# Second block's scores in two matmuls per head, with the high and low part of a value sharing the rows

## The chip, the cores and the metric

One core of a Trainium2 chip runs the whole program. The metric is device time in microseconds (us), lower is better. TensorE (PE) multiplies, VectorE (DVE) and ScalarE (ACT) do elementwise work, GpSimd (POOL) the rest, SyncE (SP) issues the transfers of the weights.

## The reference

Two models run one after the other over 256 tokens of width 2048. The change touches the second one only: two layers, each with four kinds of attention ("mixers") of eight heads of 64 columns.

```python
def second_block(x, norm_gain, w_in, q_norm_gain, k_norm_gain, forget_bias, w_out):
    for layer in range(DEPTH):
        h = rms_norm_2(x, norm_gain[layer])
        proj = jnp.einsum('bsd,dc->bsc', h, w_in[layer])
        ...
        o_a = dilated_attention(apply_rope_2(head_rms_norm(q[0], qn[0]), cos, sin), ..., v[0])
        o_b = stick_breaking_attention(q[1], k[1], v[1])
        o_c = moba_attention(apply_rope_2(head_rms_norm(q[2], qn[1]), cos, sin), ..., v[2])
        o_d = forgetting_attention(head_rms_norm(q[3], qn[2]), head_rms_norm(k[3], kn[2]), v[3], log_f)
        y = y * jax.nn.silu(gate)
        x = x + jnp.einsum('bsc,cd->bsd', y, w_out[layer])
```

## The kernel before, in words

Every operand is kept as two fp32r tiles, a high part and a low part, and a product is three matmuls (`mm3`: high by high, high by low, low by high). Weights arrive by SP's queue in pieces of 1024 columns, ACT casts each to its high part (`wh`), DVE subtracts to get the low part (`wl`).

The second block (`block2`) takes the mixers in the order 1, 0, 2, 3 (stick-breaking, dilated, moba, forgetting). In each it goes over four pairs of heads, i = 0 to 3; a pair fills the 128 partitions with two heads of 64. For every other pair `values` computes the value tiles of two pairs. `qkg` computes q, k and the gate of a pair: three products of 48 matmuls each (tile `p`, one of four PSUM tiles of that name). In mixers 0, 2 and 3 `qk` then normalizes q and k: squares on ACT, two matmuls into tile `hms` on PE, logarithm and exponential on ACT, four steps on POOL (tile `hrt`), a scaling on DVE; in mixers 0 and 2 `rope` follows (one product on POOL, four copies of 32 partitions on ACT, two steps on DVE). The result is split into a high and a low tile (`qkh`, `qkl`). So there are 8 stick-breaking pairs and 24 softmax pairs in all; 16 of those go through `rope`, 8 don't.

`attend` does the attention of a pair. The two heads share the partitions, so one operand must hold zeros where the other head is: `diag` copies parts of the high and low tile into padded tiles (`dph`, `dpl`), two copies on POOL and two on DVE each for q and for k. `soft` makes the scores (tiles `s`) in nine matmuls of 256 columns, `softmax` goes over DVE, ACT and DVE again (tile `e`), six transposes bring the probabilities back into `s`, and `split2` splits them (tile `p` of L858 and L189). The output `o` takes three matmuls of 512 columns and three of 256. `stick` has nine matmuls of 256 columns for its scores and the same six for its output. The projections back to the width of 2048 (`out_proj`, groups of 12 matmuls, `p<-yh,wh` and so on) of the mixer before stand between the pairs.

No order is written out by hand: a scheduler places each engine's instructions from the program's dependences and its own model of time, and the engines then run these lists strictly in order.

Of the kernel before, what the change touches and what calls it, by code (L numbers as in the profile page):

```python
# [9 lines left out]
F32 = mybir.dt.float32  # L10
F32R = mybir.dt.float32r
AF = mybir.ActivationFunctionType
ALU = mybir.AluOpType
# [40 lines left out]

def halves(x, n):
    return x.rearrange("p (j c) -> p j c", c=n)


def block(pair, j):
    return [t[:, j * 128:j * 128 + 128] for t in pair]  # L60


class Lazy:
# [12 lines left out]
class Net:  # L76
# [114 lines left out]
    def split(self, x, name, n, p=slice(0, 128), tag="s"):  # L191
        nc = self.nc
        h = self.slot(name + "h", F32R, tag=tag)
        l = self.slot(name + "l", F32R, tag=tag)
        nc.scalar.copy(h[p, 0:n], x)
        self.sub(l[p, 0:n], x, h[p, 0:n])
        return h, l
# [428 lines left out]
    def block2(self, l, st, rb, first_done, after):  # L626
        nc, a = self.nc, self.a
# [21 lines left out]
            return t  # L649

        NC = None
        self.diagpad(4)
        Y = {}

        def values(mx, hf):
            out = []
            ft = []
            c = 264 if mx == 3 and hf == 0 else 256
            src = a[f"vf{l}"] if c == 264 else a[f"v{l}"][(1, 0, 2, 3).index(mx) * 2 + hf - (mx == 3)]
            ws = [self.wblock(src[b], 8 * c, 4 * c) for b in range(2)]  # L660
            for tt in range(2):
                p = self.ps()[:, 0:c]
                ts = slice(tt * 128, tt * 128 + 128)
                for k in range(KD):
                    xh, xl = X[k]
                    self.mm3(p, (xh[:, ts], xl[:, ts]), self.wcol(ws[k // 8], (k % 8) * c, c), k == 0, k == KD - 1)
                if c == 264:
                    ft.append(self.small.tile([128, 8], F32, tag="ft", name="ft"))
                    nc.vector.tensor_scalar(ft[tt], p[:, 256:264], rcol()[:, tt:tt + 1], None, ALU.mult)
                p = p[:, sl]  # L670
                vh = self.slot("vh", F32R)[:, sl]
                vl = self.slot("vl", F32R)[:, sl]
                rc = rcol()[:, tt:tt + 1]
                nc.scalar.activation(vh, p, AF.Copy, scale=rc)  # L674
                nc.vector.scalar_tensor_tensor(vl, p, rc, vh.bitcast(F32), ALU.mult, ALU.subtract)
                out.append((vh, vl))
            return out, ft

        def qkg(mx, i):
# [19 lines left out]

        def attend(mx, i, q, k, g, v):  # L700
            o = self.pa("o2")
            c = slice((i % 2) * 128, (i % 2) * 128 + 128)
            hv = [[t[:, c] for t in x] for x in v]
            if mx == 1:
                p0, p1 = self.stick(q, k, masks)
            else:
                p0, p1 = self.soft(q, k, masks, NC if mx == 3 else None, i)
            self.mm3(o, hv[0], p0, True, False)
            self.mm3(halves(o, 256)[:, :, 128:256], hv[1], p1, False, True)
            yh, yl = Y[mx][i]  # L710
            t = self.slot("yt", tag="a")[:, sl]
            for j in range(2):
                R = slice(j * 64, j * 64 + 64)
                nc.vector.tensor_tensor(t[R], o[R, j * 256:j * 256 + 256], g[R], ALU.mult)
            nc.scalar.copy(yh, t)
            self.sub(yl, t, yh)

# [46 lines left out]
    def qk(self, l, mx, qk, p, rb):  # L764
        nc = self.nc
        n = SEQ
        sl = slice(0, n)
        t = self.tmp("qkt")[:, sl]
        if mx == 1:
            if qk == 0:  # L770
                nc.vector.scalar_tensor_tensor(t, p, 0.125, rb()[:, sl], ALU.mult, ALU.mult)  # L771
            else:
                nc.vector.tensor_tensor(t, p, rb()[:, sl], ALU.mult)
            return self.split(t, "qk", n)
        nc.vector.tensor_tensor(t, p, rb()[:, sl], ALU.mult)
        v = self.tmp("qsq")[:, sl]
        y = self.tmp("hry")[:, sl]
        r = self.tmp("hrt")[:, sl]
        nc.scalar.activation(v, t, AF.Square)
        vh, vl = self.tmp("qsqh", F32R)[:, sl], self.tmp("qsql", F32R)[:, sl]  # L780
        nc.scalar.copy(vh, v)
        nc.gpsimd.tensor_tensor(vl, v, vh.bitcast(F32), ALU.subtract)
        ms = self.psh.tile([128, 512], F32, tag="h", name="hms")[:, sl]
        nc.tensor.matmul(ms, self.b2const["bd64"], vh, start=True, stop=False)
        nc.tensor.matmul(ms, self.b2const["bd64"], vl, start=False, stop=True)
        self.ln(r, ms, bias=self.eps)
        nc.scalar.activation(v, ms, AF.Identity, bias=self.eps)
        nc.scalar.activation(y, r, AF.Exp, scale=-0.5)
        s = 0.125 if qk == 0 else 1.0
        nc.gpsimd.tensor_tensor(r, v, y, ALU.mult)  # L790
        nc.gpsimd.tensor_tensor(r, r, y, ALU.mult)
        nc.gpsimd.tensor_scalar(r, r, -0.5 * s, 1.5 * s, ALU.mult, ALU.add)
        nc.gpsimd.tensor_tensor(r, r, y, ALU.mult)
        gi = {0: 0, 2: 1, 3: 2}[mx]
        gcol = self.col("qk_gain", (l * 3 + gi) * 2 + qk)
        nc.vector.scalar_tensor_tensor(t, t, gcol, r, ALU.mult, ALU.mult)
        if mx == 3:
            return self.split(t, "qk", n)
        return self.rope(t, self.b2const["rope2c"], self.b2const["rope2s"], n, "qk", (v, y))

    def diagpad(self, n):

        self.dp = []
        self.dpi = 0
        for _ in range(n):
            pr = (self.slot("dph", F32R), self.slot("dpl", F32R))
            for t in pr:
                for j in range(2):
                    self.nc.gpsimd.memset(t[j * 64:j * 64 + 64, 128 - j * 128:256 - j * 128].bitcast(F32), 0.0)
            self.dp.append(pr)  # L810

    def diag(self, x, c):

        pr = self.dp[self.dpi % len(self.dp)]
        self.dpi += 1
        for t, s, eng in zip(pr, x, (self.nc.gpsimd, self.nc.vector)):
            for j in range(2):
                R = slice(j * 64, j * 64 + 64)
                eng.tensor_copy(t[R, j * 128:j * 128 + 128], s[R, c])
        return [t[:, 0:256] for t in pr]  # L820

    def soft(self, q, k, masks, NC, i):

        nc = self.nc
        s0, s1 = self.pa("s0"), self.pa("s1")
        lo, hi = slice(0, 128), slice(128, 256)
        qd = self.diag(q, hi)
        kd = self.diag(k, lo)
        if NC is not None:
            nb = self.slot("nb", F32R, [128, 512], "b")  # L830
            for j in range(2):
                h = 2 * i + j
                nc.gpsimd.tensor_scalar(
                    nb[:, j * 256:j * 256 + 256], NC.bitcast(F32), self.sel[:, h:h + 1], None, ALU.mult)
            nc.tensor.matmul(s0[:, 0:256], self.one, halves(nb, 256)[:, :, lo], start=True, stop=False)
            nc.tensor.matmul(s1, self.one, nb, start=True, stop=False)
        self.mm3(s0[:, 0:256], (q[0][:, lo], q[1][:, lo]), kd, NC is None, True)
        P = []
        for j in range(2):
            P.append([self.softmax(s0[:, j * 128:j * 128 + 128], 128, 128, masks[0])])  # L840
        for j in range(2):
            s = s1[:, j * 256:j * 256 + 256]
            self.mm3(s, block(qd, j), (k[0][:, 0:256], k[1][:, 0:256]), NC is None, NC is None or j == 1)
        for j in range(2):
            P[j].append(self.softmax(s1[:, j * 256:j * 256 + 256], 256, 128, masks[1]))
        I = self.ident
        t0, t1 = s1, s0
        for j in range(2):
            c = j * 256
            nc.tensor.transpose(t0[:, c:c + 128], P[j][0], I)  # L850
            nc.tensor.transpose(t0[:, c + 128:c + 256], P[j][1][:, lo], I)
            nc.tensor.transpose(t1[:, j * 128:j * 128 + 128], P[j][1][:, hi], I)
        return self.split2(t0, 512), self.split2(t1[:, 0:256], 256)
# [8 lines left out]
    def stick(self, q, k, masks):  # L862
# [2 lines left out]
        tri, ones = trir[:, 0:128], trir[:, 128:256]  # L865
        z0, z1 = self.pa("z0"), self.pa("z1")
        lo, hi = slice(0, 128), slice(128, 256)
        qd = self.diag(q, hi)
        kd = self.diag(k, lo)
        for j in range(2):  # L870
            self.mm3(z0[:, j * 256:j * 256 + 256], block(kd, j), (q[0][:, 0:256], q[1][:, 0:256]))
        self.mm3(z1[:, 0:256], (k[0][:, hi], k[1][:, hi]), qd)
        Z, SP = [], []
        for z, m, n in ((z0, strict0, 512), (z1[:, 0:256], strict1, 256)):
            if n == 512:
# [277 lines left out]
```

## Time and profile before

| | |
|---|---|
| time, median of 3 runs | 3187.34 us (3187.2 to 3187.79) |
| the profiled execution's own time | 3187.93 us |
| its span | 3186.2 us |
| mean granted TensorE clock | 0.999 of full speed |
| second block in the trace | 2163 to 3186 us, layers of about 511 us each |

The span runs from the first to the last instruction; 1.7 us of the time lie outside it. In the timelines below, matmuls overlap: the time that one takes in the stream is the distance from its start to the next start, not its printed duration.

### The profile page before, as it was taken

To read this page: it belongs to the slowest core of one execution; us is meant where nothing else is said; L and a number is where in the kernel's file an instruction comes from. 1 tells how busy PE (TensorE), PEld (TensorE's weight loads), DVE (VectorE), ACT (ScalarE), POOL (GpSimd) and SP (SyncE) were. 2 spreads that over 40 slices of the span, in tenths; PEclk is the share of its full clock that TensorE was granted. 3 is DMA by queue.
4 is the path that set the end of the run, shared out by engine and by line. 5 is a ranking of instruction groups with operands and counts; after the bars stand their busy time and mean duration, and the time that the engine had idled before them with its cause. 6 is when DMAs were issued, how large, how long until landed. Compare 5 with 4: busy or idle time off the path is not lost.

```text
span 3186.2 us, 64469 instructions
## 1 busy us (share of the span) xinstructions
PE 3162.5 (99%) x25987; PEld 3142.6 (99%) x25987; DVE 2161.6 (68%) x3673; ACT 1755.1 (55%) x2970; POOL 584.9 (18%) x730
## 2 busy tenths in 40 slices
PE   9999999999999999999999999999999999999999
PEld 8999999999999999999999999999999999999999
DVE  7887655555555678865555555568788778778876
ACT  6666434434344567654444444456677666666764
POOL 1001000000000133310000000023244463144453
PEclk9999999999999999999999999999999999999999
DMA  6343556556565555566565656656555555555554
GB/s 225 117 134 121 179 160 191 177 159 192 157 193 170 174 177 173 166 193 187 169 203 170 203 184 185 191 166 195 171 170 161 176 160 177 157 176 170 167 165 136
DMA packets 165693, 549.43 MB, mean 172 GB/s; under 512 B 18800, under 2 KB 38128, under 8 KB 165392
## 3 DMA queue, kind: packets, MB, share of 16 engines
q1 hardware_dynamic: 163440, 540.70, 54.5%
q0 software_dynamic: 1664, 4.33, 0.5%
q8 instruction: 203, 3.33, 0.4%
q14 instruction: 98, 0.80, 0.1%
q10 hardware_dynamic: 288, 0.27, 0.0%
HBM read 543.13 MB, written 2.10 MB: 171 GB/s over the span
## 4 chain that ended last, share of the span: by engine, by line
PE 84%; DVE 2%; issue 1%; ACT 1%; POOL 1%; DMA 1%; POOLq 0%; ACTq 0%; DVEq 0%; SPq 0%
PE p L227 27%; PE p L228 27%; PE p L226 27%; DVE wl L189 0%; DVE hs L587 0%; DMA wraw<-in 0%; PE o L228 0%; PE o L227 0%; PE o L226 0%; ACT wh L214 0%; POOL gwl L548 0%; PE s L226 0%; PE s L227 0%; PE s L228 0%; DMA gw<-lru_gate 0%
## 5 line engine op out<-in xcount | busy, mean ns | idle before, releaser
L214 ACT CAST wh<-wraw 128x1024 fp32r<-128x1024 f32 (+3 forms) x1107 | 1087.8, 984 | 977.0 <-PE p L227 751.3
L189 DVE TENSOR_TENSOR wl<-wraw,wh 128x1024 fp32r<-128x1024 f32 (+3 forms) x1107 | 1293.9, 1170 | 330.0 <-issue 253.7
L227 PE MATMUL p<-xl,wh 128*128 128x256 f32 (+1 forms) x5040 | 1430.0, 284 | 1.1 <-DVE xl L254 1.1
L226 PE MATMUL p<-xh,wh 128*128 128x256 f32 (+1 forms) x5040 | 1428.4, 283 | 0.7 <-DVE qkt L771 0.7
L228 PE MATMUL p<-xh,wl 128*128 128x256 f32 (+1 forms) x5040 | 1428.6, 283 | 0.0
L226 PEld LDWEIGHTS p<-xh,wh 128*128 128x128 f32 x5040 | 949.7, 188 | 1.7 <-ACT vh L674 0.9
L227 PEld LDWEIGHTS p<-xl,wh 128*128 128x128 f32 x5040 | 949.2, 188 | 2.0 <-DVE xl L254 1.3
L228 PEld LDWEIGHTS p<-xh,wl 128*128 128x128 f32 x5040 | 949.0, 188 | 0.5
L227 PE MATMUL p<-hidl,wh 128*128 128x272 f32 (+1 forms) x1408 | 400.7, 285 | 0.0
L228 PE MATMUL p<-hidh,wl 128*128 128x272 f32 (+1 forms) x1408 | 400.5, 284 | 0.0
L226 PE MATMUL p<-hidh,wh 128*128 128x272 f32 (+1 forms) x1408 | 400.0, 284 | 0.0
L227 PEld LDWEIGHTS p<-hidl,wh 128*128 128x128 f32 x1408 | 265.5, 189 | 0.0
L228 PEld LDWEIGHTS p<-hidh,wl 128*128 128x128 f32 x1408 | 265.2, 188 | 0.0
L226 PEld LDWEIGHTS p<-hidh,wh 128*128 128x128 f32 x1408 | 265.0, 188 | 0.0
L267 POOL TENSOR_TENSOR acc<-acc,sq 128x256 f32<-128x256 f32 (+1 forms) x81 | 76.2, 941 | 983.6 <-ACT sq L266 905.6
L226 PE MATMUL p<-yh,wh 128*128 128x256 f32 x768 | 216.1, 283 | 0.0
L228 PE MATMUL p<-yh,wl 128*128 128x256 f32 x768 | 216.0, 282 | 0.0
L227 PE MATMUL p<-yl,wh 128*128 128x256 f32 x768 | 215.8, 281 | 0.0
L267 POOL TENSOR_TENSOR accf<-accf,sq 128x256 f32<-128x256 f32 x15 | 15.9, 1063 | 703.1 <-ACT sq L266 703.1
L226 PEld LDWEIGHTS p<-yh,wh 128*128 128x128 f32 x768 | 144.5, 189 | 0.5
L227 PEld LDWEIGHTS p<-yl,wh 128*128 128x128 f32 x768 | 144.8, 189 | 0.1
L228 PEld LDWEIGHTS p<-yh,wl 128*128 128x128 f32 x768 | 144.9, 189 | 0.0
(360 smaller groups left out, 4303.9 us busy)
## 6 DMA issues: line engine op xcount, KB each, us to landing
wraw<-gu SPq DMA_DIRECT2D x352, 512.0 KB, 3.8
wraw<-dn SPq DMA_DIRECT2D x128, 512.0 KB, 3.5
wraw<-in SPq DMA_DIRECT2D x128, 512.0 KB, 4.2
wraw<-lru_in SPq DMA_DIRECT2D x64, 512.0 KB, 4.2
wraw<-g SPq DMA_DIRECT2D x64, 512.0 KB, 3.7
wraw<-out SPq DMA_DIRECT2D x64, 512.0 KB, 3.7
wraw<-v SPq DMA_DIRECT2D x56, 512.0 KB, 3.9
wraw<-dn SPq DMA_DIRECT2D x128, 192.0 KB, 2.7
```

The source lines that it names most:

```text
L189: return self.nc.vector.tensor_tensor(out, x, h.bitcast(F32), ALU.subtract)
L214: nc.scalar.copy(h[:, 0:c], raw)
L226: nc.tensor.matmul(p, lh, rh, start=first, stop=False)
L227: nc.tensor.matmul(p, lh, rl, start=False, stop=False)
L228: nc.tensor.matmul(p, ll, rh, start=False, stop=last)
L267: (eng or nc.gpsimd).tensor_tensor(st[key], st[key], s[:, 0:n], ALU.add)
```

## The change

q and k of a pair are no longer split into one high and one low tile of both heads. The operand that is loaded (q in the softmax mixers, k in stick-breaking) becomes one tile per head that has the head's 64 high rows in one half of the partitions and its 64 low rows in the other (`qks`, by `split_weights`), and a tile with the high rows in their place and zeros elsewhere (`hp`, by POOL). The operand that moves gets a tile per head with the high rows in both halves (`qkt`) and a common tile of low rows (`qkl`, by `split_moving`). The scores of a head are then two matmuls (`heads`). `diag` and its padded tiles go. The values of a head lie as high, low side by side (`vv`), so that one loaded operand gives the high and the low product in the two halves of the output's partitions, which `attend` then adds (`ol`).

```diff
         def attend(mx, i, q, k, g, v):
...
-            self.mm3(o, hv[0], p0, True, False)
-            self.mm3(halves(o, 256)[:, :, 128:256], hv[1], p1, False, True)
+            for j in range(2):
+                w0, w1 = (x[:, 2 * j:2 * j + 2].rearrange("p u c -> p (u c)") for x in hv)
+                oj = o[:, j * 256:j * 256 + 256]
+                for x in range(2):
+                    nc.tensor.matmul(oj, w0, p0[x][:, j * 256:j * 256 + 256], start=x == 0, stop=False)
+                for x in range(2):
+                    nc.tensor.matmul(oj[:, 128:256], w1, p1[x][:, j * 128:j * 128 + 128], start=False, stop=x == 1)
...
-                nc.vector.tensor_tensor(t[R], o[R, j * 256:j * 256 + 256], g[R], ALU.mult)
+                R, L = slice(j * 64, j * 64 + 64), slice(64 - j * 64, 128 - j * 64)
+                oj = o[:, j * 256:j * 256 + 256]
+                nc.scalar.copy(ol[R], oj[L])
+                nc.vector.tensor_tensor(t[R], oj[R], ol[R], ALU.add)
+            nc.vector.tensor_tensor(t, t, g, ALU.mult)
...
+    def split_weights(self, x, name, n):
...
+        for j in range(2):
+            R, L = slice(j * 64, j * 64 + 64), slice(64 - j * 64, 128 - j * 64)
+            t = self.slot(name + "s", F32R)[:, 0:n]
+            nc.scalar.copy(t[R], x[R])
+            self.sub(t[L], x[R], t[R])
+            nc.gpsimd.tensor_copy(hp[j][R, 0:n], t[R])
...
+    def split_moving(self, x, name, n):
...
+        for j in range(2):
+            R, L = slice(j * 64, j * 64 + 64), slice(64 - j * 64, 128 - j * 64)
+            t = self.slot(name + "t", F32R)[:, 0:n]
+            nc.scalar.copy(t[R], x[R])
+            self.sub(l[R], x[R], t[R])
+            nc.scalar.copy(t[L], x[R])
...
+    def heads(self, p, w, m, j, wc, mc, first, last):
+
+        nc = self.nc
+        nc.tensor.matmul(p, w[0][j][:, wc], m[0][j][:, mc], start=first, stop=False)
+        nc.tensor.matmul(p, w[1][j][:, wc], m[1][:, mc], start=False, stop=last)
...
-        self.mm3(s0[:, 0:256], (q[0][:, lo], q[1][:, lo]), kd, NC is None, True)
+        for j in range(2):
+            self.heads(s0[:, j * 128:j * 128 + 128], q, k, j, lo, lo, NC is None, NC is None or j == 1)
...
-            self.mm3(s, block(qd, j), (k[0][:, 0:256], k[1][:, 0:256]), NC is None, NC is None or j == 1)
+            self.heads(s, q, k, j, hi, slice(0, 256), NC is None, NC is None or j == 1)
...
-            self.mm3(z0[:, j * 256:j * 256 + 256], block(kd, j), (q[0][:, 0:256], q[1][:, 0:256]))
-        self.mm3(z1[:, 0:256], (k[0][:, hi], k[1][:, hi]), qd)
+            self.heads(z0[:, j * 256:j * 256 + 256], k, q, j, lo, slice(0, 256), True, True)
+        for j in range(2):
+            self.heads(z1[:, j * 128:j * 128 + 128], k, q, j, hi, hi, True, True)
```

The scheduler places the changed instructions anew. PE's list is the same up to the first scores of the second block, and SP's list is the same throughout.

Before, on PE, first softmax pair of the first layer: from k's second norm matmul (`hms`) to the first scores of the same pair 133 rows stand, all of them products for other tiles.

```order
L785 MATMUL hms<-qsql,bd_r 128x256
L226 MATMUL p<-xh,wh 128x256
...
L226 MATMUL s_28331<-dph,qkh 128x256
L226 MATMUL s_28332<-qkh,dph 128x256
L227 MATMUL s_28332<-qkl,dph 128x256
```

After the change, the same place on PE: 25 rows stand between them.

```order
L793 MATMUL hms<-qsql,bd_r 128x256
L224 MATMUL p<-xh,wl 128x256
...
L849 MATMUL s_28360<-qkt,qks 128x128
L849 MATMUL s_28361<-qkt,qks 128x256
L222 MATMUL p<-yh,wh 128x256
```

The scores have moved ahead of 108 rows that stood before them.

Before, on PE, last pair of the first layer: from the last score over the six transposes (`s<-ident,e`) to the outputs; 51 rows of other products are left out ahead of the first transpose, 8 behind it, 25 ahead of the first output and 16 behind that.

```order
L228 MATMUL s_33182<-dph,qkl 128x256
...
L850 MATMUL s_33183<-ident,e 128x128
...
L851 MATMUL s_33183<-ident,e 128x128
L852 MATMUL s_33182<-ident,e 128x128
...
L226 MATMUL o_33181<-p_33244,vh 128x512
...
L227 MATMUL o_33181<-p_33245,vh 128x512
```

After the change, the same place: nothing is left out here.

```order
L850 MATMUL s_33298<-qkl,hp 128x256
L879 MATMUL s_33298<-ident,e 128x128
L880 MATMUL s_33298<-ident,e 128x128
L881 MATMUL s_33297<-ident,e 128x128
L879 MATMUL s_33298<-ident,e 128x128
L880 MATMUL s_33298<-ident,e 128x128
L881 MATMUL s_33297<-ident,e 128x128
L710 MATMUL o_33296<-p_33350,vv 128x256
L710 MATMUL o_33296<-p_33351,vv 128x256
L712 MATMUL o_33296<-p_33354,vv 128x128
```

Scores, transposes and outputs of this pair now stand directly behind one another.

## Rows read from the trace of the kernel before

**Rows 1.** The page, first part: busy time, share of the span, instructions.

```profile
PE 3162.5 (99%) x25987; PEld 3142.6 (99%) x25987; DVE 2161.6 (68%) x3673; ACT 1755.1 (55%) x2970; POOL 584.9 (18%) x730
```

**Rows 2.** Busy time by stretch, the first layer: PE, PEld, DVE, ACT, POOL, clock, DMA share.

```profile
2163.00:2674.00 511.00, 509.05 (x4247) 505.50 (x4246) 412.73 (x810) 345.17 (x683) 212.55 (x270) 1.00 0.54 169
```

**Rows 3.** Waits of PE in the second block, the longest: total us, times, longest.

```profile
PE p L226 <- DVE qkt L771: 0.7, 1, 0.7
```

**Rows 4.** Timeline of PE, plain products: start us, duration us.

```profile
2299.85 0.27 PE L226 MATMUL p<-xh,wh 128*128 128x256 f32 x1
...
2301.98 0.28 PE L226 MATMUL p<-xh,wh 128*128 128x256 f32 x1
```

**Rows 5.** Timeline of PE, two of a pair's outputs of 512 columns.

```profile
2450.01 0.39 PE L227 MATMUL o<-p,vh 128*128 128x512 f32 x1
2450.24 0.40 PE L228 MATMUL o<-p,vl 128*128 128x512 f32 x1
```

**Rows 6.** Timeline of PE, transposes of 128 columns back to back.

```profile
2445.67 0.27 PE L852 MATMUL s<-ident,e 128*128 128x128 f32 x1
2445.78 0.27 PE L850 MATMUL s<-ident,e 128*128 128x128 f32 x1
```

**Rows 7.** Timeline of PE, first model: last of five 16-column matmuls, then full loads.

```profile
79.68 0.17 PE L455 MATMUL s<-krl,qrs 128*16 128x16 f32 x1
79.71 0.37 PE L227 MATMUL s<-kl,qh 128*128 128x256 f32 x1
79.91 0.28 PE L228 MATMUL s<-kh,ql 128*128 128x256 f32 x1
```

**Rows 8.** Timelines: k's norm matmul and k's low tile, two pairs with rope.

```profile
2322.74 0.28 PE L785 MATMUL hms<-qsql,bd_r 128*128 128x256 f32 x1
2333.93 0.43 DVE L189 TENSOR_TENSOR qkl<-qsq,qkh 128x256 fp32r<-128x256 f32 x1 [0.47 <-ACT qkh L195]
...
2295.84 0.28 PE L785 MATMUL hms<-qsql,bd_r 128*128 128x256 f32 x1
2309.66 0.43 DVE L189 TENSOR_TENSOR qkl<-qsq,qkh 128x256 fp32r<-128x256 f32 x1 [0.47 <-ACT qkh L195]
```

**Rows 9.** The same for two pairs of mixer 3, without rope.

```profile
2604.26 0.28 PE L785 MATMUL hms<-qsql,bd_r 128*128 128x256 f32 x1
2611.17 0.51 DVE L189 TENSOR_TENSOR qkl<-qkt,qkh 128x256 fp32r<-128x256 f32 x1
...
2575.44 0.28 PE L785 MATMUL hms<-qsql,bd_r 128*128 128x256 f32 x1
2585.47 0.51 DVE L189 TENSOR_TENSOR qkl<-qkt,qkh 128x256 fp32r<-128x256 f32 x1
```

**Rows 10.** Timelines of ACT, POOL and DVE behind the first matmul of rows 8.

```profile
2323.78 0.41 ACT L788 ACTIVATE hry<-hrt 128x256 f32<-128x256 f32 x1
...
2324.82 0.74 POOL L790 TENSOR_TENSOR hrt<-qsq,hry 128x256 f32<-128x256 f32 x1
...
2330.29 1.65 ACT L425 COPY hry<-qkt 32x256 f32<-32x256 f32 x4
...
2330.20 1.21 DVE L189 TENSOR_TENSOR wl<-wraw,wh 128x1024 fp32r<-128x1024 f32 x1
```

**Rows 11.** Timelines, one pair: last score, last probabilities, last transpose, their split.

```profile
2375.91 0.28 PE L228 MATMUL s<-dph,qkl 128*128 128x256 f32 x1
...
2379.34 0.62 DVE L441 TENSOR_SCALAR e<-e,rs 128x256 f32<-128x256 f32 x2
...
2382.57 0.27 PE L852 MATMUL s<-ident,e 128*128 128x128 f32 x1
...
2383.39 1.02 DVE L189 TENSOR_TENSOR p<-s,p 128x512 fp32r<-128x512 f32 x2 [0.47 <-ACT p L858]
```

**Rows 12.** Busy time by stretch in the first model, columns as in rows 2.

```profile
293.00:296.10 3.10, 1.84 (x10) 1.22 (x10) 1.34 (x4) 1.39 (x4) 0.00 (x0) 1.00 0.00 0
296.10:299.60 3.50, 3.02 (x13) 2.73 (x14) 1.24 (x4) 0.97 (x2) 0.00 (x0) 0.51 0.00 0
```

More of the change, by code (lines that the diff above doesn't have):

```diff
@@ L56, in halves @@
     return x.rearrange("p (j c) -> p j c", c=n)
-def block(pair, j):
-    return [t[:, j * 128:j * 128 + 128] for t in pair]
 class Lazy:
@@ L651, in block2 @@
         NC = None
-        self.diagpad(4)
+        self.halfpad(2)
         Y = {}
@@ L670, in values @@
                 p = p[:, sl]
-                vh = self.slot("vh", F32R)[:, sl]
-                vl = self.slot("vl", F32R)[:, sl]
                 rc = rcol()[:, tt:tt + 1]
-                nc.scalar.activation(vh, p, AF.Copy, scale=rc)
-                nc.vector.scalar_tensor_tensor(vl, p, rc, vh.bitcast(F32), ALU.mult, ALU.subtract)
-                out.append((vh, vl))
+                out.append([])
+                for i2 in range(2):
+                    v4 = halves(self.slot("vv", F32R)[:, sl], 64)
+                    vh, vl = v4[:, 0:4:3], v4[:, 1:3]
+                    pp = halves(p[:, i2 * 128:i2 * 128 + 128], 64)
+                    nc.scalar.activation(vh, pp, AF.Copy, scale=rc)
+                    nc.vector.scalar_tensor_tensor(vl, pp, rc, vh.bitcast(F32), ALU.mult, ALU.subtract)
+                    out[-1].append(v4)
             return out, ft
@@ L701, in attend @@
             o = self.pa("o2")
-            c = slice((i % 2) * 128, (i % 2) * 128 + 128)
-            hv = [[t[:, c] for t in x] for x in v]
+            hv = [x[i % 2] for x in v]
             if mx == 1:
@@ L707, in attend @@
                 p0, p1 = self.soft(q, k, masks, NC if mx == 3 else None, i)
-            self.mm3(o, hv[0], p0, True, False)
-            self.mm3(halves(o, 256)[:, :, 128:256], hv[1], p1, False, True)
+            for j in range(2):
[5 more added lines that the diff above has]
+                    nc.tensor.matmul(oj[:, 128:256], w1, p1[x][:, j * 128:j * 128 + 128], start=False, stop=x == 1)
             yh, yl = Y[mx][i]
             t = self.slot("yt", tag="a")[:, sl]
+            ol = self.tmp("ol")[:, sl]
             for j in range(2):
-                R = slice(j * 64, j * 64 + 64)
-                nc.vector.tensor_tensor(t[R], o[R, j * 256:j * 256 + 256], g[R], ALU.mult)
+                R, L = slice(j * 64, j * 64 + 64), slice(64 - j * 64, 128 - j * 64)
[3 more added lines that the diff above has]
+            nc.vector.tensor_tensor(t, t, g, ALU.mult)
             nc.scalar.copy(yh, t)
@@ L773, in qk @@
                 nc.vector.tensor_tensor(t, p, rb()[:, sl], ALU.mult)
-            return self.split(t, "qk", n)
+            return (self.split_moving if qk == 0 else self.split_weights)(t, "qk", n)
+        split = self.split_weights if qk == 0 else self.split_moving
         nc.vector.tensor_tensor(t, p, rb()[:, sl], ALU.mult)
@@ L797, in qk @@
         if mx == 3:
[L798 to L804, printed above, removed]
-        for _ in range(n):
[L806 to L820, printed above, removed]
+            return split(t, "qk", n)
+        return self.rope(t, self.b2const["rope2c"], self.b2const["rope2s"], n, "qk", (v, y), split)
@@ new lines, in halfpad @@
+    def halfpad(self, n):
+        self.hp = []
+        for _ in range(n):
+            pr = [self.slot("hp", F32R) for _ in range(2)]
+            for j, t in enumerate(pr):
+                self.nc.gpsimd.memset(t[64 - j * 64:128 - j * 64].bitcast(F32), 0.0)
+            self.hp.append(pr)
+    def split_weights(self, x, name, n):
+        nc = self.nc
+        st, hp = [], self.hp.pop(0)
+        self.hp.append(hp)
+        for j in range(2):
[4 more added lines that the diff above has]
+            nc.gpsimd.tensor_copy(hp[j][R, 0:n], t[R])
+            st.append(t)
+        return st, hp
@@ new lines, in split_moving @@
+    def split_moving(self, x, name, n):
+        nc = self.nc
+        tw = []
+        l = self.slot(name + "l", F32R)[:, 0:n]
+        for j in range(2):
[4 more added lines that the diff above has]
+            nc.scalar.copy(t[L], x[R])
+            tw.append(t)
+        return tw, l
+    def heads(self, p, w, m, j, wc, mc, first, last):
+        nc = self.nc
+        nc.tensor.matmul(p, w[0][j][:, wc], m[0][j][:, mc], start=first, stop=False)
+        nc.tensor.matmul(p, w[1][j][:, wc], m[1][:, mc], start=False, stop=last)
@@ L826, in soft @@
         lo, hi = slice(0, 128), slice(128, 256)
-        qd = self.diag(q, hi)
-        kd = self.diag(k, lo)
         if NC is not None:
@@ L867, in stick @@
         lo, hi = slice(0, 128), slice(128, 256)
-        qd = self.diag(q, hi)
-        kd = self.diag(k, lo)
         for j in range(2):
-            self.mm3(z0[:, j * 256:j * 256 + 256], block(kd, j), (q[0][:, 0:256], q[1][:, 0:256]))
-        self.mm3(z1[:, 0:256], (k[0][:, hi], k[1][:, hi]), qd)
+            self.heads(z0[:, j * 256:j * 256 + 256], k, q, j, lo, slice(0, 256), True, True)
+        for j in range(2):
+            self.heads(z1[:, j * 128:j * 128 + 128], k, q, j, hi, hi, True, True)
         Z, SP = [], []
```

## The prediction

> **What bounds the kernel now.** I read the page first: PE is busy for 99% of the span and so is its weight load [rows 1]. Since busy time is no measure of pace, I then cut the trace by stage. In the first layer of the second block PE is busy for all but 2 of 511 us, DVE for 81%, ACT for 68% [rows 2]; the second layer reads alike. The list of waits says the same from the other side: the longest that PE waits for anything in these layers is 0.7 us, once [rows 3]. So the time here is the sum of PE's slots, and whatever leaves that sum, or opens a wait in it, shows in the result. The rest of the program keeps its order and its time.
>
> A slot is read from starts. Eighteen plain products of 256 columns take 2.13 us, 0.118 us each [rows 4]. A product of 512 columns takes 0.23 us [rows 5].
>
> **What PE saves.** A pair of heads has 12 matmuls of 256 columns and 3 of 512: 12 x 0.1185 + 3 x 0.231 = 2.115 us. After the change it has 8 of 256 and 8 of 128 columns. No fp32r matmul of 128 columns against a full load stands in the trace, so its price is bounded. From below: a slot of 256 columns is 0.118 us and one of 512 is 0.113 us more, so 128 columns fewer might save half of that, down to 0.065 us. From above: 16-column matmuls have slots down to 0.03 us, but the first full load behind them shows its length. The matmul that starts at 79.71 lasts 0.37 us instead of 0.28 and the next follows 0.20 us later instead of 0.12 [rows 7]; from 79.68, where its load could begin, to its true start some 0.11 us pass. A load of 128 columns thus takes 0.11 us and can only hide behind the one matmul ahead of it. Transposes of 128 columns, each with a full load, also come every 0.11 us [rows 6]. So I take 0.109 us. Then a pair costs 8 x 0.1185 + 8 x 0.109 = 1.820 us, 0.295 us less, and 32 pairs save 9.4 us. At 0.065 us the saving would be 20.7 us.
>
> The Trainium skill gives another price: "TensorE: Matmul & The Clock Gate", section "Back-to-back issue gap", has about 81 ns for a load and a matmul of 128 columns in a stream. By that the 256 short matmuls would save 7.2 us more, 16.6 in all. The rows above show 0.11 us for the load alone, and I keep to them.
>
> **What the other engines get.** Per pair ACT has 7 instructions more (4 for splitting q and k, 1 for the values, 2 copies of `ol`), DVE about as many as before, POOL 2 fewer. At about 0.41 us each [rows 10], 16 x 7 x 0.41 = 46 us a layer come to ACT's 345 [rows 2], which fills it to 76%. That is no bound by itself. But the scheduler, with longer chains on ACT, places PE's list differently, and PE runs that list in order.
>
> **What the new order opens.** A pair's scores need k, and k's last steps start at its second `hms` matmul. In the order before, 69 to 133 other matmuls stand between the two in all 24 softmax pairs, 8.2 to 15.8 us at 0.118. The trace shows what is needed: from that matmul to the end of k's low tile 11.6 us in the quickest pair with rope and 14.2 in the slowest [rows 8], 7.4 and 10.5 us in mixer 3 [rows 9]. Cover and need fit closely, and PE does not wait. After the change I count, in us, for the pairs with rope 3.0, 12.0, 9.0, 8.4, 5.3, 12.0, 9.0, 8.9 in the first layer and 3.0, 12.0, 9.0, 6.4, 4.6, 12.0, 9.0, 6.3 in the second; for mixer 3 1.4, 0.2, 5.3, 9.5 and 1.3, 0.6, 5.3, 9.5. Behind PE's waiting matmul stands everything else, so each shortfall is lost in full, unless the need shrinks.
>
> How long is the need after the change? Without any queueing: 1.45 us from the matmul's start to the end of `hry`, four POOL steps of at most 0.74, a scaling of 0.41, for rope 1.65 and two DVE steps like the scaling, and then two ACT copies of 0.41 instead of one copy and one subtraction [rows 8, 10]: 8.1 us with rope, 5.6 without. From above: the slowest pairs, 14.2 and 10.5. I take the quickest measured pair less the one weight cast of 1.2 us that stood in its way on DVE [rows 10], since an idle PE asks for no new weights: 10.4 and 6.2 us. The shortfalls then add up to 42.9 us with rope and 23.1 without, **66 us**; by the bounds 39.5 and 148 us.
>
> The steps behind the scores lose cover too. From the end of the last score to the last probabilities 3.8 us pass, and from the start of the last transpose to the end of the split 1.8 us [rows 11]; the order before gives them 6.6 and 3 us or more. After, the sixth transpose stands 3.4 us behind the last score in eight pairs, 2.0 in two, and 0.5 in the last pair of each layer: 8 x 0.4 + 2 x 1.8 + 2 x 3.3 = 13.4 us. In four pairs the outputs stand directly behind the transposes; these lose about 1.4 us each, 5.6 us. Together **19 us**, between 10 (no cast in the way) and 30 (one more in each).
>
> Long waits cost clock as well. In the first model, after a stretch of 3.1 us in which PE was busy for 1.84, the granted clock was 0.51 for 3.5 us [rows 12], which is the lower of the two levels (1.2 instead of 2.4 GHz) and costs about 1.7 us. Twelve of the waits above are longer than 3 us: **20 us**, between 0 and 30.
>
> Sum against the profiled execution's 3187.9 us: -9.4 + 66 + 19 + 20 = +96, so 3283.5; the median of the runs shown lies 0.6 us below that execution, so **3283 us**. Nothing else is on the path: the dropped `diag` copies on POOL and DVE lay under 99% PE work, and with 0.54 of the DMA time used [rows 2] and SP's list unchanged the weights stay ahead.
>
> **Rivals.** *The chains are shorter than they look* (0.16). With PE idle the other engines run nearly free: 39.5 + 10 + 8 of clock - 9.4 = +48, 3236 us. For it speaks that every need in the trace includes queueing; against it that after the change ACT's list has more in it, in the same strict order.
>
> *The waits don't come, and the slots decide* (0.08), the other side: PE's saving stands alone, 3178 us, or 3167 with short matmuls at 0.065. It decides if k's last steps take no longer than their cover, which is 3 us at the first pair; the total of all waits would have to stay under 9.4 us. Against it: the sum of bare durations is already 8.1.
>
> *Short moving operands are slow* (0.06). If a matmul of 128 fp32r columns ran at a quarter of the pace, a slot would be as long as one of 512 columns, 0.231, and 256 of them would add 31 us to the forecast: 3314. The 16-column slots of 0.03 us [rows 7] speak against it, though not fully, since four times 16 columns would last about as long.
>
> *The waits are as long as the slowest pairs say* (0.06): +148 + 30 + 30 - 9.4, some 3380 us.
>
> **How the numbers follow.** The forecast has 0.64. The range from 3220 to 3365 holds it, the first rival and the third; outside lie the second rival and the last. Measurement tells 0.2%, 6 us, from no change: faster has the second rival's 0.08, no change 0.02 for sums that happen to meet, slower 0.90.
>
> **What the trace would show.** Second block: layers of some 560 us, with PE waiting for `qkt` and `qkl` ahead of the first scores, most at the first pair of mixer 0 (about 7 us) and the first two of mixer 3 (5 to 6), then for `e` ahead of the transposes of each layer's last pair. Slots of 128-column matmuls at 0.11 us. Granted clock below 1.00 behind the long waits. ACT's total up by about 90 us. I am wrong if PE still waits for less than 10 us there, or if the needs are much longer or shorter than 10.4 and 6.2 us.

## The result and the profile after

The changed kernel takes 3376.43 us (median of 5 runs, 3375.11 to 3377.9) against 3187.26 us for the kernel before in the same runs: 1.0594 times as long, interval 1.0583 to 1.0606. That is 189 us more, where +96 was forecast: the direction was right, and the time lies 11 us above the range.

The page's first part and the windows over the two layers of the second block stand first (columns as in [rows 1] and [rows 2]). The third window is one wait, the fourth the work right behind it.

```profile
PE 3214.8 (95%) x26019; PEld 3185.1 (94%) x26019; DVE 2192.6 (65%) x3673; ACT 1846.1 (55%) x3194; POOL 563.3 (17%) x642
```

```profile
2163.00:2765.00 602.00, 537.17 (x4275) 528.62 (x4274) 430.90 (x813) 393.54 (x799) 197.36 (x226) 0.94 0.47 144
2765.00:3373.00 608.00, 532.01 (x4227) 523.83 (x4225) 408.64 (x773) 372.68 (x756) 183.81 (x209) 0.93 0.43 138
2313.50:2323.90 10.40, 0.27 (x3) 0.06 (x2) 4.63 (x9) 5.59 (x14) 5.17 (x7) 0.62 0.31 96
2323.90:2329.70 5.80, 5.80 (x27) 5.80 (x28) 3.21 (x16) 3.98 (x13) 0.72 (x1) 0.50 0.00 1
```

The second block starts at 2163 us as before; its layers now last 602 and 608 us instead of 511 each [rows 2]. In the third window PE does nothing and no other engine is full either: that is a chain, not a busy engine. In the fourth PE is busy throughout at half clock. A mean clock of 0.94 over 602 us and 0.93 over 608 us means some 80 us at half speed in each layer, where there was none.

The waits of PE in the second block, total us, times, longest:

```profile
PE s L849 <- ACT qkt L842: 114.2, 22, 10.1
PE p L222 <- ACT yh L722: 5.5, 2, 2.7
PE p L222 <- DVE qkt L783: 3.2, 4, 1.2
PE o L710 <- ACT p L887: 2.9, 5, 0.6
```

The one large row is the wait that [rows 3] did not have: scores (L849) for k's moving tile (L842). From the starts of all matmuls the difference between the two second blocks, 1206.2 and 1019.0 us (from 2163 us to the last matmul's start), splits into parts: gaps ahead of a pair's first score 117.8 us, other gaps over 0.25 us 28 more than before, slots lengthened inside stretches of half clock 46, and PE's own slots, priced at full clock, 12 less. 7 us are spread over slots elsewhere; part of these belong to the short matmuls (see below), so the last two are best read together, 5 less. A gap read from starts is some 0.16 us longer than in the list of waits.

**Where the order comes from.** DVE in the kernel before, from the first scores of pair 0 of mixer 0 on (only the temporaries of q and k and the output `yt`):

```profile
2312.07 0.42 DVE L775 TENSOR_TENSOR qkt<-p,r2r 128x256 f32<-128x256 f32 x1
...
2317.69 0.42 DVE L775 TENSOR_TENSOR qkt<-p,r2r 128x256 f32<-128x256 f32 x1
...
2324.82 0.86 DVE L714 TENSOR_TENSOR yt<-o,gt 64x256 f32<-64x256 f32 x2 [0.45 <-PE o L228]
```

The same place after the change, ACT's first `ol` copy and then DVE:

```profile
2335.94 0.37 ACT L719 COPY ol<-o 64x256 f32<-64x256 f32 x1
```

```profile
2336.46 0.42 DVE L783 TENSOR_TENSOR qkt<-p,r2r 128x256 f32<-128x256 f32 x1
2336.79 0.40 DVE L720 TENSOR_TENSOR yt<-o,ol 64x256 f32<-64x256 f32 x1
...
2341.42 0.42 DVE L783 TENSOR_TENSOR qkt<-p,r2r 128x256 f32<-128x256 f32 x1
```

Before, the next pair's q and k were under way 12.8 and 7.1 us ahead of this pair's output. After, the next q begins 0.5 us behind this pair's first `ol` copy. In 20 of the 24 softmax pairs it begins within 1.1 us of an `ol` copy, on either side, since the two are on two engines (the expectation below says "right behind" and "in every pair", which is too strict); before, it ran up to 14 us ahead. `ol` and `qkt` are both taken by `tmp`, that is from one pool (tag "w"). This suggested the first theory below. The prediction had named another cause: longer chains on ACT.

### The profile page after: what moved, and what is told of

The parts are those of the page before. It is cut to its first block, busy times and chain, and to the rows that moved or that the text cites. A ratio compares the mean times of both kernels' runs of the same rounds, so it can differ in the third digit from the quotient of the medians.

```text
span 3373.3 us, 64725 instructions
## 1 busy us (share of the span) xinstructions
PE 3214.8 (95%) x26019; PEld 3185.1 (94%) x26019; DVE 2192.6 (65%) x3673; ACT 1846.1 (55%) x3194; POOL 563.3 (17%) x642
## 4 chain that ended last, share of the span: by engine, by line
PE 73%; POOL 6%; ACT 4%; DVE 4%; issue 3%; DMA 0%; POOLq 0%; DVEq 0%; ACTq 0%; SPq 0%
PE p L222 23%; PE p L223 23%; PE p L224 23%; POOL hrt L799 1%; POOL hrt L801 1%; ACT wh L210 1%; POOL hrt L798 1%; DVE wl L185 1%; ACT hry L421 1%; POOL hrt L800 1%; PE s L849 1%; DVE qkt L804 1%; POOL hp L828 1%; PE o L710 1%; PE s L850 0%
## 5 line engine op out<-in xcount | busy, mean ns | idle before, releaser
L222 PE MATMUL p<-yh,wh 128*128 128x256 f32 x768 | 227.5, 298 | 8.8 <-ACT yh L722 5.5
L223 PE MATMUL p<-yl,wh 128*128 128x256 f32 x768 | 224.8, 293 | 0.0
L224 PE MATMUL p<-yh,wl 128*128 128x256 f32 x768 | 224.8, 293 | 0.0
L222 PEld LDWEIGHTS p<-yh,wh 128*128 128x128 f32 x768 | 154.2, 202 | 12.9 <-ACT yh L722 5.8
L223 PEld LDWEIGHTS p<-yl,wh 128*128 128x128 f32 x768 | 154.7, 201 | 0.1
L224 PEld LDWEIGHTS p<-yh,wl 128*128 128x128 f32 x768 | 154.4, 201 | 0.0
L224 PE MATMUL p<-wh,xl 128*128 128x256 f32 (+1 forms) x512 | 145.2, 284 | 0.6 <-DVE xl L250 0.6
```

The costliest lines, as they stand in the source:

```text
L222: nc.tensor.matmul(p, lh, rh, start=first, stop=False)
L223: nc.tensor.matmul(p, lh, rl, start=False, stop=False)
L224: nc.tensor.matmul(p, ll, rh, start=False, stop=last)
```

## The experiments

Ratios are to the kernel before, measured on the same chip.

**1. `ol` from another pool.**

```diff
-            ol = self.tmp("ol")[:, sl]
+            ol = self.slot("ol", tag="a")[:, sl]
```

> The changed kernel with one word different: the temporary ol is taken from the pool that holds the probabilities (tag a) instead of the pool of temporaries (tag w) that the normalization of q and k draws on. Same instructions, same sizes. Theory 1 (the pool): in the trace of the changed kernel the temporary of the next pair's q is written right behind the first ol copy of the pair before, in every softmax pair, where before it ran ahead of that pair's outputs; ol stands in line in the same pool, so the next norm is held behind these outputs and k is late for its scores. With ol elsewhere the norm can run ahead again, 77 to 143 products stand between k's norm and its scores (9.1 to 16.9 us against needs of 7.2 to 14.1), and the waits of 118 us, the lower clock and the short tails go: 3171 us, between 3165 and 3182. Theory 2 (the chains, which the prediction named): the extra copies of the split on ACT and the hp copies on POOL are what moves the scores and makes k late; they are all still there, so the time stays at 3376, at least above 3300.

3192.34 us, 1.0015 [1.0006, 1.0024]: theory 1 by its mechanism, though 10 us above its range. One word takes 184 of the 189 us back with every instruction of the longer chains in place; theory 2 falls. Waits of PE in the second block of this kernel, the four largest:

```profile
PE p L222 <- ACT yh L722: 5.5, 2, 2.7
PE ms L1006 <- POOL accf L263: 1.7, 1, 1.7
PE hms L793 <- POOL qsql L790: 1.0, 2, 0.8
PE s L849 <- ACT qkt L842: 0.9, 3, 0.5
```

The wait for k falls from 114.2 to 0.9 us. What stays is the longer way from the last output to `yh`, 2.7 us at the end of each layer.

**2. The kernel before with its output temporary in the norm's pool.**

```diff
-            t = self.slot("yt", tag="a")[:, sl]
+            t = self.tmp("yt")[:, sl]
```

> The kernel before with one word different: the output temporary yt is taken from the pool of the norm's temporaries (tag w). No instruction is added, removed or resized, q and k are split as before. Theory 1 (the pool): the next pair's norm is held behind this pair's outputs, covers fall to 38 to 126 products with rope and 5 to 75 in mixer 3; against the needs of before (12.8 and 9.1 us on the mean) that is some 100 us of waits, with 45 for the clock and 25 behind the scores: 3357 us, between 3300 and 3390. Theory 2 (the chains): nothing changes in any chain, 3187 us.

3406.92 us, 1.0687 [1.0671, 1.0703], above even the range of theory 1: the loss is reproduced, and exceeded, without any part of the change. Its waits:

```profile
PE p L226 <- DVE gt L690: 99.5, 16, 10.3
PE s L226 <- ACT qkh L195: 33.7, 6, 6.4
```

Here products for the next `p` tile stand ahead of the scores and wait for the gate's tile to be read, which DVE does only behind k's split: the same lateness under another name.

**3 and 4. The halves of the change.** `scores_only` has the new split and `heads` with the old values and outputs, `outputs_only` has `vv` and `ol` with the old `diag` scores.

> Only the first half of the change: q and k split per head and scores in two matmuls per head; values and outputs as before (no vv, no ol). Theory 1 (the pool): no temporary of the outputs in the norm's pool, 100 to 136 products of cover with rope, 79 to 113 in mixer 3; the scores save 5 us with short slots of 0.109 us, 10.6 us at 0.065, and up to 10 us are lost in the few pairs with 100: 3177 to 3190, most likely 3180. Theory 2 (the chains): the longer chains of q and k are all here, so most of the 189 us are too, 3340 to 3376.

> Only the second half of the change: values side by side (vv), outputs added over ol from the norm's pool; q and k split and scores made as before. Theory 1 (the pool): the covers fall to 51 to 122 products with rope and 5 to 71 in mixer 3; against the needs of before the shortfalls are 83 us, with 40 for the clock and 25 behind the scores, less 6 for the slots: 3330 us, between 3290 and 3375. Theory 2 (the chains): the chains of q and k are as before, so nothing is late: 3180 to 3187.

Scores only: 3185.99 us, 0.9996 [0.9987, 1.0005], inside the range of theory 1. Outputs only: 3377.06 us, 1.0592 [1.0577, 1.0606], 2 us above the range of theory 1. The whole loss is in the half that brings `ol`, and the half with the longer chains of q and k costs nothing. Windows over the second block, scores only and then outputs only:

```profile
2163.00:3183.30 1020.30, 1014.08 (x8435) 1004.91 (x8434) 807.97 (x1522) 724.23 (x1458) 369.94 (x435) 1.00 0.54 167
```

```profile
2163.00:3377.20 1214.20, 1078.52 (x8546) 1060.43 (x8545) 852.01 (x1653) 717.60 (x1428) 396.48 (x525) 0.94 0.45 141
```

ACT is busier in the fast one (724 against 718 us).

**5 and 6. Room or line?** Two kernels tell whether `ol` takes a place that the norm lacks or stands ahead of it in a line.

```diff
-SLOTS = {"s": 66, "a": 10, "w": 11, "r": 3, "b": 5}
+SLOTS = {"s": 64, "a": 10, "w": 14, "r": 3, "b": 5}
```

> The changed kernel with 14 instead of 11 places in the pool of temporaries (and 64 instead of 66 in the largest pool, for room). A pair takes 12 temporaries for q and k, one for the gate and one for ol, 14 together. Theory 1a (the line): temporaries get their places in the order of the program, so q and k of the next pair stand in line behind ol whatever the number of places: no change, 3360 to 3385 us. Theory 1b (the room): ol holds a place that the next norm lacks; with 14 places the norm runs ahead, and the time falls to 3190 to 3230 us.

3382.81 us, 1.0612 [1.0598, 1.0627]. More room brings nothing back; the wait for k stays:

```profile
PE s L849 <- ACT qkt L842: 115.9, 22, 10.1
```

The second kernel:

```diff
...
             qk = []
+            OLS.append(self.tmp("ol")[:, sl])
+            nc.gpsimd.memset(OLS[-1][:, 0:1], 0.0)
...
-            ol = self.tmp("ol")[:, sl]
+            ol = OLS.pop(0)
```

> The changed kernel with ol in the norm's pool as it is, with 11 places as it is, but written first (one column of zeros, POOL) at the head of the pair's own q, so that its place in the line is ahead of q and k instead of behind them. 32 small memsets are added and no work is taken away. Theory 1a (the line): a temporary gets its place at its first write, in the order of the program; the next pair's q then stands behind nothing of this pair's outputs, 77 to 143 products of cover are back, and the time is that of the kernel with ol in the other pool: 3192 us, between 3187 and 3198. Theory 1b (the room): ol now holds a place of the 11 for longer, which is worse: 3376 us or more.

3192.37 us, 1.0013 [1.0004, 1.0022], the time of experiment 1, and the wait for k is gone:

```profile
PE s L851 <- ACT qkt L844: 0.9, 3, 0.5
```

With the same pool and the same 11 places a one-column write at the right point of the program takes 184 us off. The line it is: places in the pool go in program order, and later temporaries wait behind an earlier one that has none yet. The edit moves both the call that asks for `ol` and its first write; which of the two sets its place in the line is not told apart here. In the changed kernel both come when the pair's outputs are done, so the next pair's q could not start before.

**7. The clock.** Zeros for PE to multiply, where it waited.

```diff
...
+        with self.tc.issue_after(self.khms.ins):
+            for _ in range(FILL.pop(0)):
+                nc.tensor.matmul(s1, self.zero[:, 0:128], self.zero, start=True, stop=True)
...
```

> The changed kernel with work added for PE alone: behind k's second norm matmul of each softmax pair stand as many 512-column matmuls of zeros (0 to 47, 548 in all; their result is overwritten by the scores) as fill the wait that the trace showed there, nearly to its end. Everything else is placed as in the changed kernel, but for up to 22 products more or fewer in some pairs (about +4 us in all). Theory: 118 us of the loss are waits for k and some 50 us the lower clock that follows them (157 us at half speed in the trace). With PE kept busy over the waits the clock stays at 1.00, the waits themselves are not shortened: 3330 us, between 3315 and 3345, with a granted clock of 0.99 or more. Rival (the clock costs what the prediction said, 20 us, and the rest is more waiting for k and for the probabilities): 3355 to 3362 us.

3357.42 us, 1.0531 [1.0516, 1.0545] (the zeros are 516 matmuls, not 548 as counted there). The second block and its two largest waits:

```profile
2163.00:3355.90 1192.90, 1148.76 (x9024) 1070.58 (x9022) 826.39 (x1587) 763.13 (x1555) 369.24 (x436) 0.99 0.45 143
```

```profile
PE s L851 <- ACT qkt L844: 9.7, 5, 3.3
PE s L885 <- DVE e L437: 8.0, 10, 1.4
```

The clock stays up as the theory said, 0.99 in place of 0.94 and 0.93, but only 19 us come back; in time the rival was right. From the starts of all matmuls: slots lengthened by half clock fall from 46 to 9 us, zeros and remaining gaps ahead of the scores are 118 us together, as much as the gaps were, and 19 us are lost anew: gaps elsewhere grow from 32 to 43 us (transposes now wait 8.0 us for `e`) and slots at full clock lose 8 more. This fits a PE at half speed that had been covering part of the waits that follow; no run takes that apart.

**8. `hp` on DVE.**

```diff
-            nc.gpsimd.tensor_copy(hp[j][R, 0:n], t[R])
+            nc.vector.tensor_copy(hp[j][R, 0:n], t[R])
```

> The changed kernel with the two hp copies of each loaded operand moved from POOL to DVE. In the trace q's two hp copies (1.1 to 1.9 us together) stand on POOL between the first and the second of k's four norm steps. Theory (the need for k is long because q's own chain stands in k's way): each k is ready 1.1 to 1.9 us sooner, less 0.4 where DVE's copies get in the way; in the 22 softmax pairs that wait some 24 us go, and about 5 us of clock: 3348 us, between 3335 and 3362. Rival (weight casts on ACT and DVE set the pace of the chain, POOL has slack): no change, 3370 to 3380 us.

3371.82 us, 1.0573 [1.0559, 1.0588], 5 us less than the changed kernel: the rival's number. In the changed kernel the two copies stand between k's first and second step in 13 of the 22 pairs that wait, not in each. POOL in the third pair of mixer 0, the changed kernel and then this one:

```profile
2391.62 0.73 POOL L798 TENSOR_TENSOR hrt<-qsq,hry 128x256 f32<-128x256 f32 x1 [2.15 <-ACT hry L796]
2392.29 1.14 POOL L828 CAST hp<-qks 64x256 fp32r<-64x256 f32 x2
2393.51 1.59 POOL L799 TENSOR_TENSOR hrt<-hrt,hry 128x256 f32<-128x256 f32 x1
...
2395.68 1.69 POOL L801 TENSOR_TENSOR hrt<-hrt,hry 128x256 f32<-128x256 f32 x1
```

```profile
2391.31 0.73 POOL L798 TENSOR_TENSOR hrt<-qsq,hry 128x256 f32<-128x256 f32 x1 [2.13 <-ACT hry L796]
2392.12 0.80 POOL L799 TENSOR_TENSOR hrt<-hrt,hry 128x256 f32<-128x256 f32 x1
...
2393.50 0.79 POOL L801 TENSOR_TENSOR hrt<-hrt,hry 128x256 f32<-128x256 f32 x1
```

POOL's four steps take 3.0 instead of 5.8 us here, 1.1 us of it for the copies that are gone and 1.7 because two steps run shorter (see the last section), but the next links (DVE among them) give half of it back: PE's wait in this pair falls from 3.4 to 1.9 us. In the ten of those 13 pairs that have the same number of products as cover in both kernels, the time from k's second `hms` to the first score falls by 0.5 to 1.5 us, 1.1 on the mean: what the theory said for one pair. Pairs in which the new order left fewer products as cover wait longer (5.3 to 8.4 us in the fourth), so that over all pairs with rope the mean falls by 0.4 us only. The rival has the number by this trade, and POOL did not have slack in those pairs.

**9. The end of each layer.** `ol` from the other pool, and two groups of 12 products held back in the last pair.

```diff
...
+                    with self.tc.issue_after(self.last["to"[m4 - 2]].ins) if held and mb == 3 and m4 > 1 else ExitStack():
-                    self.gemm(p, w, Y[mx], sl, m4 * 512)
+                        self.gemm(p, w, Y[mx], sl, m4 * 512)
...
```

> The changed kernel with ol from the pool of the probabilities, and 24 products of the third projection held back in each layer: 12 behind the last transpose of the last pair, 12 behind its last output. In the trace of the kernel with that pool PE waits 2.9 us behind the last output of each layer, for the longer way over ol and yt to yh, and the clock falls for 3.4 us behind one of them. Theory: these waits go, 5.8 us and about 1.7 us of clock, and some 0.8 us is lost ahead of the outputs: 3192 less 6.7 = 3185.6 us, between 3182 and 3190. Rival (the wait only moves ahead of the transposes or the outputs): 3191 to 3195 us.

3186.98 us, 0.9998 [0.9989, 1.0007]: as expected, 5.4 us better than experiment 1, and the waits for `yh` are gone. This whole change, repaired, and its first half alone (experiment 3) both end within 0.1% of the kernel before; none beats it by what can be measured.

## Why the prediction was right in direction and wrong in size

**What bounds the kernel.** Right. PE's slots were the time, and nearly all that was put between them shows: 22 waits of 114 us are the largest part of the loss.

**The sum.** The forecast is 93 us short. The waits for k took 118 us instead of 66, the clock 46 instead of 20, other gaps 28 instead of 19, and the slots gave 5 back instead of 9 (12 less 7, as split above).

**PE's saving.** Right. Predicted 0.109 us for a short matmul and -9.4 us. In the kernel of experiment 1, at full clock, two short scores stand between plain products:

```profile
2470.45 0.39 PE L849 MATMUL s<-qkt,qks 128*128 128x128 f32 x2
2470.68 0.28 PE L222 MATMUL p<-xh,wh 128*128 128x256 f32 x1
```

Two take 0.23 us, 0.115 each. Start to start the recorded slot can read 0.06 with the following one 0.17, so only stretches count that begin and end in plain products. An estimate from some 620 such stretches without gaps at full clock (a least-squares fit) gives 0.109 to 0.113 us, give or take 0.003, in the kernels of experiments 1, 6 and 9, and -9 us for the change. The quarter-pace rival fell. The Trainium skill's 81 ns ("TensorE: Matmul & The Clock Gate", section "Back-to-back issue gap") is lower; the measurement decides. These 9 us do not become time: in experiment 9 the gaps of PE in the second block add up to 5.6 us instead of 2.6 before, and where the rest went is open.

**ACT's share.** Size right (1755 to 1846 us, +91), consequence wrong. The sentence "the scheduler, with longer chains on ACT, places PE's list differently" is refuted by experiments 1 and 3: the rows that the prediction counted were moved by the line in the pool of temporaries. The forecast did not need the cause, as it took the covers from the new order. But without it the remedy would have been sought in the chains.

**The waits for k.** This is the step that failed: needs of 10.4 and 6.2 us, 66 us in all. Measured from k's second `hms` to the first score: 11.8 to 14.2 us with rope, mean 13.4, and 7.3 to 9.0 in the six pairs of mixer 3 that wait, mean 8.3; 114 to 118 us in all (by the list of waits and by starts). The prediction took the quickest pair of before and subtracted a weight cast "since an idle PE asks for no new weights". The 24 chains of before, from k's second `hms` to the end of its low tile, take 12.8 us on the mean with rope and 9.1 in mixer 3; with these needs the prediction's own list of covers gives 115 us. The chain in the first pair with rope, from the changed kernel:

```profile
2310.47 0.28 PE L793 MATMUL hms<-qsql,bd_r 128*128 128x256 f32 x1
...
2311.11 1.65 ACT L421 COPY hry<-qkt 32x256 f32<-32x256 f32 x4 [2.31 <-DVE qkt L804]
...
2312.79 1.05 ACT L210 CAST wh<-wraw 128x1024 fp32r<-128x1024 f32 x1
...
2313.74 0.47 ACT L133 ACTIVATE hrt<-hms,eps 128x256 f32<-128x256 f32 x1
...
2314.95 0.72 POOL L798 TENSOR_TENSOR hrt<-qsq,hry 128x256 f32<-128x256 f32 x1 [2.14 <-ACT hry L796]
...
2315.62 1.93 POOL L828 CAST hp<-qks 64x256 fp32r<-64x256 f32 x2
...
2317.63 0.78 POOL L799 TENSOR_TENSOR hrt<-hrt,hry 128x256 f32<-128x256 f32 x1
...
2323.41 0.40 ACT L842 CAST qkt<-qsq 64x256 fp32r<-64x256 f32 x1
...
2323.87 0.48 PE L849 MATMUL s<-qkt,qks 128*128 128x128 f32 x1 [10.13 <-ACT qkt L842]
```

k's logarithm (L133) stands 3.3 us behind its matmul, because q's four rope copies and a weight cast come first on ACT. Then q's `hp` copies take 1.93 us between k's first and second step on POOL. PE stood idle from 2313.7 us on, and none of this went away: a second weight cast began on ACT at 2315.61. Over the eight pairs with rope of the first layer, POOL's four steps take 5.4 us on the mean, against 2.6 for their four durations here, and 3.0 us pass up to the end of `hry` where the first rows of [rows 10] allow 1.45: that is most of the 5 us between the bare sum of 8.1 and the 13.4 measured. Of the 2.8 us on POOL 1.8 are the four steps themselves, which ran longer than in this pair (the last section has why), and 0.8 are `hp` copies that stand between them in five of the eight pairs. The prediction counted only that POOL has 2 instructions fewer.

**Behind the scores.** Predicted 19 us, bounds 10 to 30; other gaps grew by 28 us. Within the bounds. The expected wait for `e` in the last pair is there, the larger one is for `yh` (2.7 us per layer), which was not named: `ol` and its additions lengthen that way.

**The clock.** Predicted 20 us from twelve waits of 1.7 us; too small as a term. By slots it is 46 us: the granted clock fell to half (1.2 GHz) 21 times in the two layers, for 3.4 to 13.7 us each, in or behind 19 of the 22 waits for k and at the end of each layer. The three waits without a fall are of 1.9 to 2.0 us, and one of 2.0 us has a fall. The run in which the clock hardly fell was 19 us faster. That the number lies near this net value is luck: the prediction did not think of what the slow slots cover.

**Rivals.** The one that came nearest in time was "as long as the slowest pairs" (0.06, "some 3380 us"; its terms add up to 3386), with fewer waits for k than its 148 us and more clock than its 30. "The chains are shorter than they look" and "the waits don't come" fell: the chains were longer than forecast.

## What to carry to other kernels

A small temporary that is asked for and first written late may sit in a line ahead of the next group's first temporaries; when an order changes for no visible reason, look whether the next group's first write comes right behind the new tile's, and try another pool, or an earlier place in the program, before shortening any chain. Where two halves of a change can be run apart, run them apart: here one half cost 0 and the other 190 us. For the length of a chain that an idle engine waits for, take the mean of what measured chains took, with all that stands ahead in each engine's list, not the bare durations and not the quickest chain.

## What the runs showed that was not expected

POOL's steps have two durations. In the second pair of mixer 0 of the changed kernel the same step L801 takes 0.74 us for q and 1.58 us for k:

```profile
2345.35 0.74 POOL L801 TENSOR_TENSOR hrt<-hrt,hry 128x256 f32<-128x256 f32 x1
...
2355.21 1.58 POOL L801 TENSOR_TENSOR hrt<-hrt,hry 128x256 f32<-128x256 f32 x1
```

DVE, from the same stretch:

```profile
2346.12 0.49 DVE L804 SCALAR_TENSOR_TENSOR qkt<-qkt,cols,hrt 128x256 f32<-128x256 f32 x1 [2.65 <-POOL hrt L801]
```

```profile
2351.87 4.33 DVE L185 TENSOR_TENSOR wl<-wraw,wh 128x1024 fp32r<-128x1024 f32 x3
```

Ahead of 2346.12 DVE had been idle for 2.65 us; from 2351.87 to 2356.20 it ran three weight subtractions, and POOL's step beside the third took twice as long. The Trainium skill ("GPSIMD Engine Reference", section "Key points") says that GpSimd shares its SBUF interfaces with VectorE and that the two contend when a VectorE instruction has two SBUF inputs. A weight subtraction has two, and the trace agrees; the order of the starts decides who pays. One step and one subtraction of the same trace, POOL first by 0.09 us:

```profile
2462.74 0.74 POOL L801 TENSOR_TENSOR hrt<-hrt,hry 128x256 f32<-128x256 f32 x1
```

```profile
2462.83 1.73 DVE L185 TENSOR_TENSOR wl<-wraw,wh 128x1024 fp32r<-128x1024 f32 x1 [1.27 <-PE p L224]
```

The second block of the changed kernel has 144 such steps (L798, L799 and L801). The 65 with no weight subtraction beside them take 0.72 to 0.80 us, the 24 that begin ahead of one 0.73 to 0.80, and the 55 that begin while one runs 0.94 to 1.73. A subtraction of 1024 columns takes 1.20 to 1.23 us where no POOL instruction ran when it began, and up to 1.80 where one did. So of the two the one that starts first keeps its own time and the other waits. No run was made without the subtractions.
